# A weight-gradient matmul on one core: one load in four pieces, whole stores, a split last visit and a new hand-written order

## The chip, the cores and the metric

The kernel runs on one core of a Trainium2 chip. The core has five engines that run side by side, each through its own list of instructions: TensorE (PE in the profile; its weight loads are PEld) multiplies matrices into PSUM, VectorE (DVE) and ScalarE (ACT) add, copy and round, GpSimd (POOL) here adds a little and issues loads that change the number format, and SyncE (SP) issues plain transfers. Sixteen DMA engines move data between the chip's large memory (HBM) and the core's SBUF. PSUM has eight banks, and a matmul of this kernel fills three quarters of one.

The metric is the device time of one execution in microseconds (us); lower is better. The runs before took 161.19, 161.51 and 161.19 us.

## The reference

```python
batch, m, k, n = 16, 512, 1024, 768
# input [batch, m, k] and grad_output [batch, m, n], float32
grad_weight = np.einsum('bmk,bmn->kn', input, grad_output)   # [k, n] = [1024, 768]
```

With X the input as an 8192 x 1024 matrix and G the gradient as 8192 x 768, the result is X-transposed times G: a sum over 8192 rows. 58.7 MB are read and 3.1 MB are written.

## The kernel before

**Tiles.** The rows are cut into 64 slices of 128. X's columns are two halves of 512, each four quarters of 128 (q = 0 to 3); G's are two halves of 384 (LEFT, RIGHT). A product of one quarter (128 x 128, the weights) and one half of G (128 x 384) is one matmul of 384 columns, the only shape of line L331. The result's four blocks are A (first half of X, LEFT), B (first, RIGHT), C (second, LEFT) and D (second, RIGHT), each in four quarters.

**Two kinds of load.** The first eight slices (kind "s") are multiplied plainly, 16 matmuls a slice. The other 56 go in 28 pairs of slices (kind "P"), where VectorE makes sums and differences of the half tiles (`sum_x`, `sum_g`, lines L184 to L198), so that seven products (A, B, C, 1, 5, 6, 7) replace eight: 28 matmuls a pair. In all 8 x 16 + 28 x 28 = 912 matmuls. Products 1, 5, 6 and 7 are collected in their own sums (`macc`) and added to the blocks at the end.

**Loads.** Nearly all loads are issued by POOL (L153, L154, L158, L160) and rounded to bfloat16 on the way. Slice 0 and the X part of slice 1 come as float32 over the hardware queues: G's halves (`gf`) from SP (L128, L130), X of slice 0 (`xf[0]`) and of slice 1 (`xf[1]`) from ScalarE's queue (L129, L131). `round_by` (L202) then rounds them, partly on VectorE, partly on ScalarE; the tokens `r0` to `r4` place five of these: r0 is the right half of G of slice 0 (VectorE), r1 and r2 are quarters of X of slice 1 (VectorE), r3 and r4 the others (ScalarE). Meanwhile TensorE runs 17 warm-up matmuls on constants (L136).

**The order by hand.** The scheduler is off for TensorE, VectorE, ScalarE and POOL. `PLAN`, a list of some 1200 tokens, gives the order, and each engine runs its own tokens in that order:

- `C0@2.1`: begin block C, quarter 0, in bank 2 and run one matmul; `C0.1` runs one more there. `@R` means the block's own resident bank (5, 6, 7 for A0, A1, A2). Such a stretch in one bank is called a visit.
- `fB1@1`: fill bank 1 with what B1 has so far (ScalarE copy, L309), so that the next visit adds to it.
- `vB1`, `cB1`, `kC1`: close the visit. `v` is VectorE (a copy L376, an add L378, a last add L371 or L364 and L366), `c` a ScalarE copy to SBUF (L356), `k` an add by VectorE that folds D in (L360).
- `g0.4`, `x0.4`: stages of the sums of pair 4.
- `pA3`, `qA0`: POOL adds the shared sum (L388); `q` stores the block after it.

A bank can be begun or filled again only when the engine that closes it has read it. A closing with a last add stores its block: `store` (L285 to L291) issues one transfer of 128 x 384 (192 KB) on SP's queue, or, for the first four stores (`HALVED`), two of 96 KB. There are 16 such blocks, so 20 transfers.

Of the kernel before, what the change touches and what calls it, by code (L numbers as in the profile page):

```python
# [9 lines left out]
P = 128  # L10
# [4 lines left out]
    "C0@2.1 A0@R.1 r0 r1 r3 B1@1.1 r2 A2@R.1 r4 A1@R.1 vB1 A1.1 D3@4.2 A0.1 C0.1 D0@3.1 B2@0.1 cC0 B2.1 D0.1 "  # L15
    "fB1@1 A2.1 B3@2.2 cD3 B1.2 B3.1 D2@4.1 cB1 D2.1 vB3 D2.1 D0.1 A0.1 C1@2.3 C2@1.4 A1.2 cC2 B2.1 C1.1 B2.1 "
    "D2.1 cC1 D1@1.2 vD2 D1.1 fD3@2 D1.1 A2.2 cD0 vD1 B0@4.1 D3.2 A3@3.2 cD3 A3.2 B0.2 vA3 B0.1 C3@1.4 B2.2 "
    "B1@3.1 B0.1 cB2 B0.1 A1.2 cB0 D2@0.2 A0.3 D0@2.3 C3.2 A2.1 C0@4.1 vC3 C0.3 B1.2 B3@1.5 B1.1 D0.1 C0.1 vB1 "
    "C0.1 A0.2 vB3 D0.1 fD3@3 D2.2 vC0 fC3@1 A2.3 vD0 fD1@4 D3.3 vD2 D3.1 D1.1 g0.4 D1.1 fC1@0 D1.2 C3.1 fA3@2 "
    "g1.4 C3.1 C1.1 vD1 cD3 C1.3 kC3 fC2@3 A3.2 g2.4 A3.1 fB2@1 A3.1 x0.4 A3.1 C2.2 cA3 C2.1 x1.4 C2.2 A2.1 "  # L20
    "x2.4 10@2.1 cC2 A0.1 C1.1 v10 12@4.1 60@3.1 cC1 B2.1 g0.5 B2.1 c12 B2.1 61@0.1 g1.5 c60 62@2.1 B0@4.1 vB2 "
    "B0.1 c61 B0.1 11@3.1 c62 A1.1 vB0 A1.1 f12@1 A1.1 13@0.1 x0.5 13.1 12.1 11.1 c13 73@4.1 x1.5 73.1 c11 "
    "50@2.2 c12 k73 51@0.1 53@3.1 c50 53.1 x2.5 A1.1 52@4.1 g0.6 c53 52.1 51.1 fB1@2 A0.1 v52 63@1.2 c51 "
    "71@3.1 g1.6 71.1 fC0@4 g2.5 B1.2 g2.6 B1.1 c63 70@0.1 k71 70.1 C0.1 f10@1 C0.1 x0.6 C0.1 c70 B3@3.2 A1.1 "
    "cC0 10.1 x1.6 10.1 cB1 72@0.1 vB3 72.1 c10 72.1 C1@4.1 x2.6 f62@3 C1.1 60@2.1 k72 60.1 cC1 61@1.2 g0.7 "
    "A0.1 fB2@4 62.1 v61 62.1 B0@0.2 c62 g1.7 B2.2 vB0 c60 C3@1.2 cB2 C3.1 g2.7 C2@3.2 x0.7 fA3@2 C2.1 12@0.1 "
    "f51@4 12.1 vC3 A3.2 cC2 A3.1 v12 51.2 cA3 70@1.1 x1.7 70.1 c51 53@0.1 g0.8 53.1 A2.1 c70 A2.1 x2.7 A2.1 "
    "fB3@2 A1.1 v53 63@4.1 fB1@1 63.1 B3.1 g1.8 B3.1 f11@3 13@0.1 v63 13.1 cB3 B1.2 g2.8 11.1 v13 C3@4.1 cB1 "
    "C3.1 A2.1 x0.8 fC1@2s 11.2 C0@1.1 f71@0 C0.1 vC3 C1.2 cC0 71.1 x1.8 71.1 c11 71.1 vC1 52@1.2 c71 52.1 "
    "g0.9 A1.1 f73@3 60@4.2 v52 50@2.1 f62@0 50.1 g1.9 50.1 f13@1 73.1 v60 73.2 c50 62.1 x2.8 62.1 72@4.1 g2.9 "  # L30
    "72.1 c62 10@2.1 x0.9 10.1 c73 10.1 13.2 f70@0s v10 A0.2 f51@3 A0.1 v72 70.2 c13 51.1 x1.9 51.1 fC2@4s "
    "61@2.1 v70 61.1 fB2@1 61.1 C2.1 x2.9 C2.1 c51 B0@0.1 g0.10 B0.1 c61 B0.1 B2.1 vC2 B2.1 f11@3 B2.1 A2.1 "
    "vB0 f71@4 A3@2.2 x0.10 A3.1 cB2 11.1 A0.1 f12@0 11.1 g1.10 A2.1 71.1 f63@1 vA3 71.1 12.1 c11 12.1 g2.10 "
    "12.1 x1.10 c71 A1.2 g0.11 63.1 c12 63.2 fB1@4 x2.10 C1@3.2 g1.11 c63 62@2.2 vC1 B1.2 fB3@1 B1.1 v62 "
    "C0@0.1 fC3@3 C0.1 B3.1 g2.11 B3.1 cB1 B3.1 x0.11 C3.2 f72@4 C3.1 vC0 13@2.2 cC3 A2.1 x1.11 72.1 cB3 72.1 "
    "v13 72.1 f50@3s 73@0.2 g0.12 73.1 f53@1 52@2.2 v73 52.1 c72 50.2 g1.12 50.1 f60@0s 53.1 v52 53.1 fC0@4s "
    "53.2 g2.12 60.1 f51@2 v50 60.2 c53 A1.1 x0.12 A0.2 fB2@3 A1.1 C0.1 v60 f10@1 51.3 x1.12 C0.1 f70@0 10.2 "
    "vC0 c51 10.1 70.2 g0.13 70.1 f61@4s C2@2.2 x2.12 c70 C2.1 61.1 x2.11 c10 61.2 vC2 B2.2 f11@1 B2.1 g1.13 "
    "B0@0.1 f12@2 v61 B0.2 11.2 vB0 f62@4 11.1 12.2 cB2 x0.13 12.1 A3@0.1 c11 A3.2 g2.13 C1@3.1 f71@1 x1.13 "
    "C1.2 vA3 62.1 c12 62.2 g0.14 71.1 f63@0 71.2 x2.13 fC3@2 A2.1 63.1 vC1 63.1 c71 63.1 C3.1 g1.14 C3.1 c63 "  # L40
    "A2.1 g2.14 B3@1.1 c62 B3.2 x0.14 C3.1 A0.2 cC3 vB3 53@4.3 fB1@2 x1.14 73@0.2 v53 73.1 f72@1 50@3.2 x2.14 "
    "50.1 B1.1 v73 72.3 v50 60@4.2 c72 60.1 g0.15 B1.1 f52@0 B1.2 v60 13@3.3 A1.1 f70@4 x0.15 A1.2 cB1 52.2 "
    "v13 52.2 70.1 g1.15 70.1 c52 x1.15 70.1 A2.1 fC2@3 A2.1 g2.15 C0@0.1 g0.16 C0.1 c70 C0.1 C2.1 fB2@2 x2.15 "
    "C2.2 vC0 B0@4.2 cC2 B2.1 g1.16 B2.2 fC1@3 g2.16 51@1.2 vB0 51.1 cB2 12@0.2 x0.16 12.1 f10@4 C1.3 v51 10.2 "
    "cC1 10.1 x1.16 10.1 61@2.1 v12 61.1 c10 61.2 x2.16 f11@1 A1.1 71@0.1 g0.17 71.1 fB3@4 71.1 v61 62@3.3 v71 "
    "B3.3 v62 53@2.2 cB3 B1@0.1 g1.17 B1.1 11.1 v53 11.3 vB1 f60@2 A3@4.3 x0.17 c11 A3.1 A2.1 f72@3 A2.1 vA3 "
    "50@0.1 70@1.2 g0.18 72.1 f13@4 72.1 50.1 x1.17 50.1 72.1 v70 13.2 c72 13.1 g1.18 60.2 g2.17 c13 60.1 v50 "
    "63@1.1 fB2@3 63.2 g2.18 63.1 f73@0 A0.1 x0.18 A0.1 f52@4 A0.2 73.1 c60 x1.18 73.2 x2.17 73.1 52.1 x2.18 "
    "63.1 c73 C0@2.2 v63 C0.1 B0@0.2 vC0 B0.2 52.1 g0.19 52.1 fA3@2 A1.2 vB0 c52 B2.3 g1.19 f61@4 10@1.1 x0.19 "
    "10.2 A3.2 g2.19 51@0.2 x1.19 cA3 51.2 v10 cB2 A2.1 61.2 f62@2 v51 61.1 C1@3.2 x2.19 fC2@0 C1.1 62.1 g0.20 "  # L50
# [12 lines left out]
    "C2.2 vB0 C3@2.1 B2.1 A1.1 g1.27 fC0@4 A1.1 kC2 C3.3 g2.27 C3.1 f72@0 C0.2 x0.27 C0.3 vC3 71.3 kC0 72.1 "
    "fC1@2 72.2 vB2 72.1 fA3@4 72.2 x1.27 C1.2 c72 v71 C1.3 g0.28 f73@0 62@1.3 fB3@3 kC1 62.1 A0.1 73.1 g1.28 "
    "73.1 f51@2 v62 73.2 A3.1 g2.28 A3.2 x0.28 A3.1 52@1.2 cA3 51.1 x2.27 51.1 c73 51.1 x1.28 51.2 52.1 A1.1 "
    "50@0.1 v52 50.3 v51 61@4.1 f70@1 61.2 g0.29 61.2 70.1 g1.29 70.2 v61 70.1 A2.1 A1.1 v50 B3.1 f63@4 12@2.2 "
    "x0.29 12.1 63.3 x1.29 A2.2 g2.29 A2.1 70.1 x2.28 63.1 A0.1 v12 A0.2 B3.1 k70 B3.2 B1@0.1 x2.29 B1.1 cB3 "
    "B1.1 g0.30 B1.1 c63 B1.1 10@2.2 x0.30 f60@4 10.4 vB1 60.2 53@3.1 g1.30 53.2 x1.30 53.2 g2.30 13@0.2 v53 "
    "13.2 60.2 g0.31 f72@3 A1.2 f11@1 v10 A0.1 A2.1 72.1 g1.31 72.1 f12@2 72.1 11.1 g2.31 11.1 x2.30 11.2 "
    "x0.31 11.2 A1.1 13.1 c11 13.1 x1.31 12.1 cA1 12.1 v13 12.1 A0.1 f62@1 A2.1 x2.31 10@6.1 p63 c12 72.1 60.1 "  # L70
    "v10 cA2 62.3 cA0 62.1 v60 63@7.1 f73@6 63.1 qA0 v62 A3@0.1 f70@4 A3.1 73.1 v63 73.1 f50@5 73.2 qA2 v72 "
    "70.1 f53@2 A3.1 50.1 v73 70.1 fC3@3 53.1 50.1 v70 f61@1 qA1 50.1 C3.2 v53 fC2@7 C3.2 fB3@6 C3.1 pA3 61.2 "
    "cC3 61.1 v50 C2.1 f71@4 C2.3 qC3 f51@3 C2.1 v61 71.2 cC2 71.1 vA3 71.1 fC0@1 B3.1 qC2 B3.1 v71 B3.1 fB1@7 "
    "51.2 vB3 f52@0 51.1 C0.1 pC1 C0.1 fB0@4 v51 C0.2 fB2@5 C1@2.4 vC0 B1.2 52.1 vC1 52.2 vB1 B2.3 v52 B2.2 "
    "B0.4 vB2 B0.2 vB0 "
).split()

WARMUP = [("b", 512), ("f", 512), ("f", 512)] + 14 * [("b", 128)]
PAIRS_HELD = 11
SUMS_HELD = 8  # L80
MERGED = 2
HALVED = 4
ASIDES = 7
# [5 lines left out]
def kernel(  # L89
# [6 lines left out]
    nc = tc.nc  # L96
    bf16 = mybir.dt.bfloat16
    f32 = mybir.dt.float32
# [242 lines left out]
    def close(engine, p, q, queue):  # L341
# [39 lines left out]
        if last(p, q) and not opened[p, q] and not (engine == "c" and p in "ABC"):  # L381
            closed.add((p, q))
# [66 lines left out]
```

## Time and profile before

| what | value |
|---|---|
| runs, us | 161.19, 161.51, 161.19 (median 161.19) |
| profiled execution, us | 161.48 |
| its span (first to last instruction), us | 159.70 |
| granted TensorE clock | 0.999 |
| HBM read, over the span | 58.72 MB |
| TensorE: matmuls of L331, first and last start, us | 912; 5.91 and 155.75 |
| one whole VectorE closing (128x384), mean | 0.55 us |
| one ScalarE fill or closing, mean | 0.48 to 0.49 us |
| one POOL add (L388), mean | 1.0 us |
| SP's store issues, first to last end, us | 147.16 to 157.03 |
| issue to landing of a store, median, us | 2.1 (192 KB), 1.7 (96 KB) |

A row of the timeline or of the groups is one kind of instruction at one line: start, busy time, engine, line, operation, what it writes and reads, how many, and in brackets the idle time before it with what ended it. Matmuls overlap, so their busy time is longer than the step from one to the next. The row of a window gives, for each engine, the busy time and the number of instructions in that stretch, then the clock, the busy share of the DMA engines and what they moved. A cast load counts there with the bytes that it writes, which are half of those read.

### The profile page before, as it was taken

The page shows a single profiled execution, that of the slowest core. Times are in us where ns is not written, and L with a number is a line of the kernel's source. Part 1 is how long each engine was busy: PE and PEld are TensorE (multiplying, and loading weights), DVE is VectorE, ACT ScalarE, POOL GpSimd, SP SyncE. Part 2 cuts the span into 40 slices and gives each one's busy share as a digit, 9 for nine tenths or more (in the row PEclk, how much of TensorE's full clock was granted, in tenths as well). Part 3 has the DMA queues.
Part 4 walks back from the last instruction along what each step waited for, and adds up shares of the span by engine and source line. Part 5 has one row for each costly group of instructions (what it writes and reads, how often), then busy time and mean ns, then how long its engine had stood idle before and what let it go on. Part 6 is the DMA issues. An engine that isn't in the chain of part 4 may idle for free.

```text
span 159.7 us, 2734 instructions
## 1 busy us (share of the span) xinstructions
PE 154.6 (97%) x931; PEld 91.2 (57%) x931; DVE 136.1 (85%) x316; ACT 104.4 (65%) x243; POOL 42.6 (27%) x77
## 2 busy tenths in 40 slices
PE   8899999999999999999999999999999999999990
PEld 3456656556555565665656565656566565656560
DVE  0514169999999999999999999989999899999992
ACT  3445238999999999967867585563465472339930
POOL 7442222222212222221222221222222100006930
PEclk9999999999999999999999999999999999999999
DMA  5999999999999999999999999999999999940696
GB/s 171 297 212 211 214 216 212 213 213 212 213 213 211 214 212 213 214 211 214 213 214 212 214 213 214 212 211 213 213 211 219 208 214 213 213 81 0 196 353 239
DMA packets 12829, 33.40 MB, mean 209 GB/s; under 512 B 1424, under 2 KB 4624, under 8 KB 12816
## 3 DMA queue, kind: packets, MB, share of 16 engines
q0 software_dynamic: 9360, 28.64, 90.7%
q1 hardware_dynamic: 3168, 3.54, 6.6%
q10 hardware_dynamic: 288, 1.05, 1.7%
q8 instruction: 7, 0.11, 0.3%
q14 instruction: 6, 0.05, 0.1%
HBM read 58.72 MB, written 3.15 MB: 387 GB/s over the span
## 4 chain that ended last, share of the span: by engine, by line
PE 91%; DMA 4%; DVE 2%; issue 1%; ACT 0%; ACTq 0%; DVEq 0%
PE bank L331 91%; DMA xf<-in_input_dram 4%; DVE acc L371 1%; DVE macc L364 0%; DVE xp L202 0%; ACT macc L356 0%; ACTq L129 0%; DVE acc L378 0%; DVE acc L366 0%; DVEq L371 0%
## 5 line engine op out<-in xcount | busy, mean ns | idle before, releaser
L331 PE MATMUL bank<-gp,xp 128*128 128x384 bf16 x576 | 105.4, 326 | 0.7 <-DVE xp L202 0.6
L331 PEld LDWEIGHTS <-xp 128*128 128x128 bf16 x576 | 55.8, 98 | 39.1 <-DVE xp L202 1.0
L331 PE MATMUL bank<-ge,xe 128*128 128x384 bf16 x336 | 65.9, 326 | 0.0
L331 PEld LDWEIGHTS <-xe 128*128 128x128 bf16 x336 | 32.7, 98 | 22.3 <-DVE xe L184 0.6
L309 ACT COPY bank<-macc 128x384 f32<-128x384 f32 x69 | 32.6, 489 | 10.4 <-DVE macc L378 6.2
L356 ACT COPY macc<-bank 128x384 f32<-128x384 f32 x64 | 29.4, 484 | 10.4 <-PE bank L331 10.1
L378 DVE TENSOR_TENSOR macc<-bank,macc 128x384 f32<-128x384 f32 x56 | 30.5, 554 | 1.2 <-PE bank L331 0.9
L154 POOL DMA_DIRECT2D xp<-in_input_dram x30 | 15.9, 529 | 52.6 <-DMA xp<-in_input_dram 21.9
L309 ACT COPY bank<-acc 128x384 f32<-128x384 f32 x46 | 21.8, 485 | 11.5 <-DVE acc L378 8.9
L356 ACT COPY acc<-bank 128x384 f32<-128x384 f32 x44 | 20.7, 480 | 11.4 <-PE bank L331 11.1
L153 POOL DMA_DIRECT2D gp<-in_grad_output_dram x30 | 15.9, 531 | 38.4 <-PE bank L331 17.2
L378 DVE TENSOR_TENSOR acc<-bank,acc 128x384 f32<-128x384 f32 x42 | 22.8, 553 | 1.9 <-PE bank L331 1.9
L184 DVE TENSOR_TENSOR xe<-xp 128x1024 bf16<-128x1024 bf16 x28 | 19.3, 689 | 1.0 <-DMA xp<-in_input_dram 0.9
L194 DVE TENSOR_TENSOR ge<-gp 128x768 bf16<-128x768 bf16 x28 | 15.5, 552 | 0.2 <-DMA gp<-in_grad_output_dram 0.2
L376 DVE COPY acc<-bank 128x384 f32<-128x384 f32 x9 | 5.0, 555 | 8.9 <-PE bank L331 8.9
L186 DVE TENSOR_TENSOR xe<-xe,xp 128x512 bf16<-128x512 bf16 x28 | 11.8, 421 | 0.3
L188 DVE TENSOR_TENSOR xp<-xp,xe 128x512 bf16<-128x512 bf16 x28 | 11.5, 419 | 0.0
L196 DVE TENSOR_TENSOR ge<-gp,ge 128x384 bf16<-128x384 bf16 x28 | 9.9, 353 | 0.2
L198 DVE TENSOR_TENSOR gp<-ge,gp 128x384 bf16<-128x384 bf16 x28 | 9.8, 354 | 0.2
L388 POOL TENSOR_TENSOR acc<-acc,macc 128x384 f32<-128x384 f32 x7 | 6.8, 1003 | 0.5 <-ACT acc L356 0.5
L388 POOL TENSOR_TENSOR macc<-macc 128x384 f32<-128x384 f32 x1 | 1.0, 1042 | 18.0 <-DVE macc L378 18.0
L202 DVE CAST gp<-gf 128x192 bf16<-128x192 f32 (+1 forms) x2 | 0.6, 310 | 4.9 <-DMA gf<-in_grad_output_dram 4.9
(23 smaller groups left out, 41.2 us busy)
## 6 DMA issues: line engine op xcount, KB each, us to landing
xp<-in_input_dram POOLq DMA_DIRECT2D x30, 512.0 KB, 16.7
gp<-in_grad_output_dram POOLq DMA_DIRECT2D x30, 384.0 KB, 16.7
out_dram<-acc SPq DMA_DIRECT2D x12, 192.0 KB, 2.1
xf<-in_input_dram ACTq DMA_DIRECT2D x2, 512.0 KB, 4.9
out_dram<-acc SPq DMA_DIRECT2D x8, 96.0 KB, 1.7
gp<-in_grad_output_dram POOLq DMA_DIRECT2D x3, 192.0 KB, 6.4
xp<-in_input_dram POOLq DMA_DIRECT2D x2, 256.0 KB, 7.8
gf<-in_grad_output_dram SPq DMA_DIRECT2D x2, 192.0 KB, 4.1
```

The costliest lines, as they stand in the source:

```text
L153: nc.gpsimd.dma_start(out=gp, in_=G[rows, :].rearrange("(p m) n -> p m n", m=2))
L154: nc.gpsimd.dma_start(out=xp, in_=X[rows, :].rearrange("(p m) k -> p m k", m=2))
L184: nc.vector.tensor_sub(out=xe[:, 0:2, :], in0=x[:, 1::-1, :], in1=x[:, 3::-2, :])
L186: nc.vector.tensor_sub(out=xe[:, 2, :], in0=xe[:, 0, :], in1=x[:, 0, :])
L188: nc.vector.tensor_add(out=x[:, 1, :], in0=x[:, 2, :], in1=xe[:, 2, :])
L194: nc.vector.tensor_add(out=ge[:, 0:2, :], in0=g[:, 0:2, :], in1=g[:, 1::2, :])
L196: nc.vector.tensor_add(out=ge[:, 2, :], in0=g[:, 3, :], in1=ge[:, 0, :])
L198: nc.vector.tensor_add(out=g[:, 1, :], in0=ge[:, 2, :], in1=g[:, 2, :])
L309: nc.scalar.copy(out=tile_[:, at : at + c1 - c0], in_=src[:, c0:c1])
L331: nc.tensor.matmul(tile_[:, at : at + c1 - c0], stat, mov[:, c0:c1], start=fresh, stop=True, skip_group_check=True,)
L356: nc.scalar.copy(out=to, in_=b)
L378: nc.vector.tensor_add(out=to, in0=b, in1=to)
```

## The change

Five things are changed together.

1. X of slice 1 (`xf[1]`) is loaded in four transfers of 32 rows each, alternately on ScalarE's and SP's queue, instead of one of 128 rows on ScalarE's.
2. The first of the warm-up matmuls writes bank 4, the others bank 7; before, all wrote bank 7.
3. No store is halved (`HALVED = 0`).
4. The last visit, of B2, is split over two banks, 256 columns in bank 7 and 128 in bank 1 (`fB2@7+1`). Each part is closed and stored by itself, the first on SP's queue, the second on ScalarE's. The kernel before already had the code for such a visit, and did not use it at the end.
5. `PLAN` is another order of the same 912 matmuls. It has 128 instead of 129 VectorE closings by `v`, 119 instead of 115 ScalarE closings, 124 instead of 122 fills, six `q` and two `p` instead of five and three. Three lines of `close` allow a ScalarE closing of a block that POOL has prepared; no token of the new order needs them.

```diff
 PLAN = (
-    "C0@2.1 A0@R.1 r0 r1 r3 B1@1.1 r2 A2@R.1 r4 A1@R.1 vB1 A1.1 D3@4.2 A0.1 C0.1 D0@3.1 B2@0.1 cC0 B2.1 D0.1 "
...
-    "70.1 f53@2 A3.1 50.1 v73 70.1 fC3@3 53.1 50.1 v70 f61@1 qA1 50.1 C3.2 v53 fC2@7 C3.2 fB3@6 C3.1 pA3 61.2 "
-    "cC3 61.1 v50 C2.1 f71@4 C2.3 qC3 f51@3 C2.1 v61 71.2 cC2 71.1 vA3 71.1 fC0@1 B3.1 qC2 B3.1 v71 B3.1 fB1@7 "
-    "51.2 vB3 f52@0 51.1 C0.1 pC1 C0.1 fB0@4 v51 C0.2 fB2@5 C1@2.4 vC0 B1.2 52.1 vC1 52.2 vB1 B2.3 v52 B2.2 "
-    "B0.4 vB2 B0.2 vB0 "
+    "A0@R.1 C2@2.1 A3@3.1 A2@R.1 cC2 A1@R.1 vA3 C0@1.1 C1@0.1 vC1 r3 r0 r2 D2@4.1 r1 D2.1 vC0 B0@2.2 B1@0.2 "
+    "cB0 D1@1.2 r4 C3@3.3 D2.1 A1.1 cC3 A1.1 vD2 A2.1 cB1 A2.1 B3@2.2 fC1@0 B3.1 C0@3.2 fA3@4 C1.2 vC0 C1.1 "
...
+    "f72@6 61.1 qA2 61.1 v70 50.1 cA0 50.2 f52@0 v61 53.1 72.1 fB3@7 72.1 qC0 v50 72.2 fC3@3 52.2 B3.1 f71@5 "
+    "B3.1 v72 qA0 C3.1 fC2@2 C3.2 v53 C3.1 cB3 C3.1 71.1 f51@4 71.1 qB3 71.1 v52 cC3 71.2 C2.1 fB2@7+1 C2.2 "
+    "qC3 C2.1 v71 C2.1 fC1@0 51.2 vC2 fB1@3 51.1 C1.2 v51 fB0@6 C1.2 B1.2 B0.2 vB1 B0.3 vC1 B0.1 B2.2 vB0 B2.5 "
+    "vB2 "
 ).split()
...
-HALVED = 4
+X1_PARTS = 4
+HALVED = 0
...
-    nc.scalar.dma_start(out=xf[1], in_=X[P : 2 * P, :])
-
-    wps = psum.tile([P, 512], f32, name="bank7")
-    for dt, cols in WARMUP:
+    if X1_PARTS == 1:
+        nc.scalar.dma_start(out=xf[1], in_=X[P : 2 * P, :])
+    else:
+        n = P // X1_PARTS
+        for b in range(X1_PARTS):
+            engine = nc.scalar if b % 2 == 0 else nc.sync
+            engine.dma_start(out=xf[1][b * n : (b + 1) * n, :], in_=X[P + b * n : P + (b + 1) * n, :])
+
+    warm = [psum.tile([P, 512], f32, name=f"bank{b}") for b in (4, 7)]
+    for n, (dt, cols) in enumerate(WARMUP):
         dtype = f32 if dt == "f" else bf16
         nc.tensor.matmul(
-            wps[:, 0:cols],
+            warm[min(n, 1)][:, 0:cols],
...
+                assert (p, q) not in prepared or (final and carried and len(parts) == 1)
...
-        if last(p, q) and not opened[p, q] and not (engine == "c" and p in "ABC"):
+        if final and engine == "c" and (p, q) in prepared:
+            store(p, q, 0, NH, queue)
+        if last(p, q) and not opened[p, q] and (engine != "c" or p not in "ABC" or (p, q) in prepared):
             closed.add((p, q))
```

Between the removed and the added lines that end the list, the last visit before is B0's with two matmuls and one closing; after, it is B2's with five matmuls in each of two banks.

## The prediction

> **What bounds the kernel now.** I read the page's busy shares first, then windows of the span, then single waits on the timeline, then the stores.
>
> ```profile
> PE 154.6 (97%) x931; PEld 91.2 (57%) x931; DVE 136.1 (85%) x316; ACT 104.4 (65%) x243; POOL 42.6 (27%) x77
> ```
>
> TensorE has 97%. The 912 matmuls of L331 start between 5.91 and 155.75 us, and nearly all steps from one to the next in the trace are 162 or 163 ns: 911 steps of 0.1626 are 148.13 of 149.84 us. So 1.71 us is idle, and a new order can only win there and at the two ends. The windows (busy us and count of PE, PEld, DVE, ACT, POOL; clock, DMA share, GB/s) show a second bound:
>
> ```profile
> 2.00:3.00 1.00, 1.00 (x3) 0.46 (x2) 0.00 (x0) 0.95 (x1) 1.00 (x3) 1.00 0.87 254
> 3.00:4.00 1.00, 1.00 (x3) 0.35 (x2) 0.00 (x0) 0.00 (x0) 1.00 (x2) 1.00 1.01 407
> 6.00:7.00 1.00, 0.96 (x7) 0.30 (x4) 0.36 (x1) 0.00 (x0) 0.00 (x0) 1.00 1.13 241
> 12.00:40.00 28.00, 28.00 (x174) 16.52 (x174) 20.33 (x45) 19.67 (x47) 6.86 (x13) 1.00 1.07 213
> 120.00:140.00 20.00, 20.00 (x124) 11.85 (x123) 18.75 (x46) 9.05 (x21) 1.58 (x3) 1.00 1.07 213
> ```
>
> From 3 us until the last load lands (142.53 by the landing record of that load) the 16 DMA engines are never free. TensorE runs just behind them, and the idle spots show it:
>
> ```profile
> 7.70 20.16 PE L331 MATMUL bank<-gp,xp 128*128 128x384 bf16 x123 [0.62 <-DVE xp L202]
> ...
> 11.92 15.55 PEld L331 LDWEIGHTS <-xp 128*128 128x128 bf16 x97 [0.21 <-DMA xp<-in_input_dram]
> ...
> 51.79 0.60 PEld L331 LDWEIGHTS <-xp 128*128 128x128 bf16 x5 [0.34 <-DMA xp<-in_input_dram]
> ...
> 88.41 0.48 ACT L356 COPY macc<-bank 128x384 f32<-128x384 f32 x1 [0.62 <-PE bank L331]
> ...
> 125.73 0.69 DVE L184 TENSOR_TENSOR xe<-xp 128x1024 bf16<-128x1024 bf16 x1 [0.70 <-DMA xp<-in_input_dram]
> ```
>
> In steps over 0.1626, the idle 1.71 us is: 0.78 before the sixth matmul (slice 1) and 0.20 before the third (right half of G of slice 0); 0.12 at 51.5 and 0.16 at 126.2 behind loads; the remaining 0.45 where a bank or a sum came late (0.15 at 40.1, 0.25 at 88.5, small ones).
>
> Then the end, where nothing but stores is left:
>
> ```profile
> 149.00:150.00 1.00, 1.00 (x8) 0.61 (x7) 1.00 (x4) 1.00 (x4) 1.00 (x3) 1.00 0.65 206
> 150.00:151.00 1.00, 1.00 (x8) 0.59 (x7) 1.00 (x4) 1.00 (x4) 0.98 (x2) 1.00 0.65 207
> 152.00:153.00 1.00, 1.00 (x9) 0.59 (x7) 1.00 (x3) 1.00 (x3) 1.00 (x2) 1.00 1.02 364
> 156.00:157.00 1.00, 0.08 (x1) 0.00 (x0) 0.65 (x2) 0.00 (x0) 0.00 (x0) 1.00 1.02 363
> 157.00:158.00 1.00, 0.00 (x0) 0.00 (x0) 0.00 (x0) 0.00 (x0) 0.00 (x0) 1.00 1.03 369
> ```
>
> The halved stores move 206 GB/s; the whole ones fill the DMA engines from 152 to 158.3. The eight halves leave SP at 147.16 to 150.43, about 0.48 apart; whole ones at 151.00 to 154.90, about 0.49 apart. 192 KB at 366 GB/s is 0.54 us, so whole stores land 0.54 apart, and the last at 158.80: 151.00 + 1.35 until data flow + 12 x 0.54 = 158.8. So the last 7 us hang on the store stream from 151.0 on, and the last adds of VectorE only have to keep up with it.
>
> **The change, part by part.** Sum against the profiled execution's 161.48 us (span 159.70, 1.78 around it). The runs shown have a median of 161.19, so this execution lies 0.29 above it.
>
> *Opening.* The built order on TensorE is seven matmuls of slice 0 with the left half of G, then D2, which needs the right half. VectorE rounds that half (r0) only behind two copies of banks, of A3 (third matmul) and C1 (seventh). First matmul at 5.91 (it follows the warm-up, whose 17 matmuls are unchanged; one of them writes another bank and no later instruction comes sooner by that: 0). C1 starts 6 x 0.1626 later, at 6.89; a VectorE reader of a bank starts 0.36 after the matmul's start (last one: 155.75 to 156.12): 7.25; r0 follows at the pitch of 0.465 of such copies: 7.72, ends 0.36 later (row of the 128x384 rounding): 8.08; D2 8.10. Behind r0 wait r2, r1 and the copy of C0; TensorE needs them at 8.4, 9.1 and 9.1 and has them at 8.3, 8.5 and 9.0. In the kernel before the eighth matmul starts at 8.03: +0.07. Then the 31st matmul, at 8.10 + 23 x 0.1626 = 11.84, needs slice 3, which landed at 11.88: +0.06. Opening: +0.13, in place of the waits of 0.78 and 0.20.
>
> *X of slice 1 in four.* It landed at 7.12. Now r2 is at its turn at 7.99 and ScalarE's r3 is needed by 7.8, so an earlier landing wins nothing and up to 0.6 later costs nothing itself. The bytes, and the 16 engines, are the same, with a share of 1.01 to 1.16 already in 3 to 8 us; two more issues of 0.43 each lie on SP (empty until 147) and on ScalarE, whose table load then ends at 3.4, before its first rounding at 4.22. I take 0 for the loads behind it. Below: 0 too, since the free share of 2 to 3 us lies before any piece could start. Above: 512 KB at 400 GB/s are 1.3 us; at half that rate, 1.3 us more.
>
> *New order.* It has the same 912 matmuls, one VectorE closing less, two ScalarE fills and four ScalarE closings more. I counted where each load is first needed, at 0.1626 a matmul. The load of 51.75 is first used by the 276th matmul instead of the 275th, that of 125.70 by a VectorE sum nine matmuls later (736th against 727th): -0.28. Tightest now is the load of 47.44, due 47.42 with the opening's shift: +0.05. Late banks and sums: 0.45 before, not countable by slack; bounds 0 and 0.9, I take 0.45, since closings and fills number nearly the same and ScalarE (65% busy) has room for six copies of 0.48. Middle: -0.23.
>
> *Last visit split.* B2's last seven matmuls become seven of 256 and seven of 128 columns. The last 128-column matmuls of the warm-up start 57 ns apart, its 14 cost 96 ns on average; 256 columns lie between 57 and 163 (110 taken). The last start moves from 6 x 0.163 to 7 x 0.110 + 6 x 0.058 behind the visit's first: +0.14 (up to +0.4 at 96). What it shortens, the last add and store, is hidden by the store stream: without that cover the add of 0.55 would fall to some 0.25.
>
> *No store halved, new end.* Behind B3's last matmul come 30 whole matmuls and B2's 14 parts, so it starts 31 x 0.1626 + 1.12 = 6.16 before the last start, T. ScalarE copies B3 after 0.36 + 0.38 (behind a fill) in 0.48, POOL adds in 1.0 (its rows: 1003 ns), SP stores 0.03 later: T - 3.91. Ten stores' worth (nine whole, one in 128 + 64 KB) follow, all ready when SP gets to them at 0.49 apart: T - 3.91 + 1.35 + 10 x 0.54 = T + 2.84. Before, the last landing was 158.80 - 155.75 = 3.05 behind the last start: -0.21. The four stores made whole save 4 x 0.47 us of SP, but POOL's adds, 1 us apart, hide most of that.
>
> Sum: +0.13 - 0.23 + 0.14 - 0.21 = -0.17, so 161.31 against the profiled execution; from the median, without the late load that other executions need not have (-0.16), it is 161.19 + 0.16 - 0.17 = 161.18. I take **161.2 us**: no change. One measurement can tell about 0.2% (0.32 us) from none, so this means 160.87 to 161.51.
>
> **Rivals.** *Pieces of 32 rows load slowly (slower).* Each piece writes a quarter of the partitions. If that goes at half rate, and two of the four pieces find no other transfer to run beside, 0.65 us of the load stream is lost. For: the share above 1 leaves nothing to make it up, and loads are used as they land: slice 2 (9.63) is due 9.72, slice 3 has no slack. Against: every transfer of the trace has 128 rows, so no row shows it. It decides from 0.1 us on: 161.2 + 0.65 - 0.1 = 161.75, up to 162.4.
>
> [...]
>
> *The new order hands banks over later (slower).* VectorE is busy 85% and stays so; twice the 0.45: 161.65. Against: as many closings.
>
> *The new order has no late banks (faster).* TensorE then follows the loads: the last, at 142.53, is first used by the 834th matmul, 78 steps and the split before T: 142.55 + 12.68 + 0.14 = 155.37, last landing 158.21, 0.59 less than 158.80; 160.6 to 160.9 after the two reference times: 160.75. For: the order is set by load times everywhere else. Against: the wait at 88.4 came with a copy whose matmul was long done, which no order excludes.
>
> **How the numbers follow.** Forecast 0.40, slow pieces 0.26, late banks 0.10, no late banks 0.24. So faster 0.24, the same 0.40, slower 0.36. The range takes the fast case and most of the slow pieces: 160.7 to 161.9; the forecast's own is 160.87 to 161.51.
>
> **What would show it.** Right: the eighth matmul at 8.1 behind r0; X of slice 1 landed before 7.8 and that wait gone from the chain; loads of slices 2 and 3 at 9.6 and 11.9; no wait at 126; DMA share 1.0 from about 152 to 158, last landing 2.8 to 2.9 behind the last matmul's start. Wrong: slices 2 and 3 later by 0.2 or more (slow pieces), an eighth matmul before 7.8, idle TensorE over 0.9 us in the middle, or a share under 0.9 in the last 5 us, which would put the end back on the last add.

## The result, and the profile after

The changed kernel took 162.37 us (median of 12 executions, beside 161.38 for the kernel before): 1.0069 times as long, interval 1.0055 to 1.0083. A second series gave 162.30 against 161.38, 1.0060 (1.0046 to 1.0074). It is slower by 0.6 to 0.7%, above the forecast of 161.2 and outside its range.

The first profiled execution, of 164.81 us, has a disturbance of its own: TensorE's clock fell to 0.50 for 3.4 us. Two of the first twelve executions (163.92 and 164.81) show a lower mean clock (0.985 and 0.99), the other ten (0.995 to 1.00) take 162.07 to 162.41. TensorE's rows on its timeline, and its windows (columns as in the prediction):

```profile
5.75 1.60 PE L338 MATMUL bank<-gp,xp 128*128 128x384 bf16 x7 [0.50 <-DVE xp L209]
8.27 0.32 PE L338 MATMUL bank<-gp,xp 128*128 128x384 bf16 x1 [0.91 <-DVE gp L209]
10.13 4.62 PE L338 MATMUL bank<-gp,xp 128*128 128x384 bf16 x17 [1.54 <-ACT xp L209]
```

```profile
9.00:10.00 1.00, 0.00 (x0) 0.00 (x0) 0.29 (x1) 0.33 (x1) 0.53 (x1) 1.00 1.14 209
...
11.00:12.00 1.00, 1.00 (x4) 0.45 (x3) 0.00 (x0) 0.61 (x2) 0.53 (x1) 0.50 1.14 213
12.00:13.00 1.00, 1.00 (x4) 0.45 (x3) 0.00 (x0) 0.04 (x1) 0.53 (x1) 0.50 1.12 217
13.00:14.00 1.00, 1.00 (x5) 0.46 (x4) 0.56 (x1) 0.97 (x3) 0.53 (x1) 0.50 1.10 217
```

Seven matmuls, a wait, one matmul, a longer wait, and then four matmuls per us instead of eight at a clock of 0.50. The fall costs 1.7 us (eleven steps of 0.32 instead of 0.163). Whatever is said of the change from here on is read from an execution of the second series, 162.26 us at a clock of 0.995. Its page and its timeline:

```profile
span 160.4 us, 2757 instructions
...
PE 153.9 (96%) x938; PEld 92.0 (57%) x938; DVE 136.4 (85%) x316; ACT 107.5 (67%) x250; POOL 42.5 (26%) x77
...
PE bank L338 92%; DMA xf<-in_input_dram 4%; DVE acc L379 0%; SPq L138 0%; SPq L131 0%; ACT xp L209 0%; SPq L129 0%; DVEq L454 0%; ACTq L209 0%
```

```profile
5.68 1.30 PE L338 MATMUL bank<-gp,xp 128*128 128x384 bf16 x7
...
7.89 0.32 PE L338 MATMUL bank<-gp,xp 128*128 128x384 bf16 x1 [0.91 <-DVE gp L209]
8.80 0.41 ACT L209 CAST xp<-xf 128x256 bf16<-128x256 f32 x1 [2.12 <-DMA xf<-in_input_dram]
8.84 0.50 DVE L209 CAST xp<-xf 128x256 bf16<-128x256 f32 x2 [1.00 <-DMA xf<-in_input_dram]
...
9.26 0.66 PE L338 MATMUL bank<-gp,xp 128*128 128x384 bf16 x3 [1.04 <-ACT xp L209]
```

The chain of waits, in order of time, shows the same from the other side, first in the kernel before, then in the changed one:

```profile
1.18 5.94 DMA xf<-in_input_dram
7.12 0.02 issue
7.14 0.51 DVE xp L202 x2
```

```profile
1.65 0.42 SPq L138
2.07 0.04 issue
2.11 6.53 DMA xf<-in_input_dram
...
8.80 0.41 ACT xp L209
9.22 0.05 issue
9.26 34.55 PE bank L338 x211
43.81 0.03 issue
43.83 112.53 PE bank L338 x695
```

In the kernel before, the whole tile lands at 7.12. In the changed one SP issues its first piece at 1.65 to 2.07 (the first row) and its second, the last of the four, from 2.11 on; that one lands at 8.64. VectorE and ScalarE stand idle until then (the 1.00 and 2.12 in brackets) and round it, and the ninth matmul starts at 9.26. From there TensorE runs almost without a stop to the end: the time is lost once, in the first 10 us. The ninth matmul starts 1.06 us later than in the kernel before (8.20) and the last one 0.65 later; the difference is later waits that the new order does not have.

| landings and starts, us | before | changed | changed, first profile |
|---|---|---|---|
| right half of G of slice 0 | 6.00 | 6.42 | 7.06 |
| X of slice 1 whole | 7.12 | 8.64 | 9.51 |
| X of slice 2, of slice 3 | 9.63, 11.88 | 10.28, 12.48 | 10.94, 13.14 |
| last matmul starts | 155.75 | 156.41 | 158.96 |
| last store lands | 158.80 | 159.42 | 161.98 |
| end of the span | 159.71 | 160.39 | 162.95 |

### The profile page after: what moved, and what is told of

The parts are those of the page before. It is cut to its first block, busy times and chain, and to the rows that moved or that the text cites. A ratio compares the mean times of both kernels' runs of the same rounds, so it can differ in the third digit from the quotient of the medians.

```text
span 162.9 us, 2757 instructions
## 1 busy us (share of the span) xinstructions
PE 155.3 (95%) x938; PEld 92.4 (57%) x938; DVE 136.3 (84%) x316; ACT 107.6 (66%) x250; POOL 42.6 (26%) x77
## 4 chain that ended last, share of the span: by engine, by line
PE 91%; DMA 5%; SPq 1%; DVE 0%; issue 0%; ACT 0%; DVEq 0%; ACTq 0%
PE bank L338 91%; DMA xf<-in_input_dram 5%; DVE acc L379 0%; SPq L138 0%; SPq L131 0%; ACT xp L209 0%; SPq L129 0%; DVEq L454 0%; ACTq L209 0%
## 5 line engine op out<-in xcount | busy, mean ns | idle before, releaser
L338 PE MATMUL bank<-gp,xp 128*128 128x384 bf16 (+2 forms) x583 | 106.5, 328 | 3.1 <-ACT xp L209 1.5
L338 PEld LDWEIGHTS <-xp 128*128 128x128 bf16 x583 | 57.2, 99 | 41.9 <-ACT xp L209 3.4
L338 PE MATMUL bank<-ge,xe 128*128 128x384 bf16 x336 | 64.9, 326 | 0.0
L316 ACT COPY bank<-macc 128x384 f32<-128x384 f32 x66 | 31.3, 487 | 11.2 <-DVE macc L386 6.8
L386 DVE TENSOR_TENSOR macc<-bank,macc 128x384 f32<-128x384 f32 x59 | 32.1, 552 | 2.4 <-PE bank L338 1.8
L364 ACT COPY macc<-bank 128x384 f32<-128x384 f32 x62 | 28.8, 483 | 7.9 <-PE bank L338 7.3
L316 ACT COPY bank<-acc 128x384 f32<-128x384 f32 (+2 forms) x52 | 24.6, 482 | 12.4 <-DVE macc L386 7.1
L364 ACT COPY acc<-bank 128x384 f32<-128x384 f32 x50 | 23.3, 481 | 11.1 <-PE bank L338 10.8
L386 DVE TENSOR_TENSOR acc<-bank,acc 128x384 f32<-128x384 f32 x40 | 21.9, 553 | 8.6 <-PE bank L338 8.5
L384 DVE COPY acc<-bank 128x384 f32<-128x384 f32 x8 | 4.4, 553 | 4.2 <-PE bank L338 4.1
L379 DVE TENSOR_TENSOR macc<-bank,macc 128x384 f32<-128x384 f32 x7 | 3.7, 551 | 0.0
```

The lines of the kernel that those rows point to most:

```text
L316: nc.scalar.copy(out=tile_[:, at : at + c1 - c0], in_=src[:, c0:c1])
L338: nc.tensor.matmul(tile_[:, at : at + c1 - c0], stat, mov[:, c0:c1], start=fresh, stop=True, skip_group_check=True,)
L364: nc.scalar.copy(out=to, in_=b)
L386: nc.vector.tensor_add(out=to, in0=b, in1=to)
```

## The experiments

Times are medians with the ratio to the kernel before and its 95% interval. "End" is the time from the last landing to the end of the span in the run's profile; what sets it is told with the last group.

| kernel | us | ratio (interval) | end |
|---|---|---|---|
| before | 161.35 to 161.40 | | 0.91 |
| changed | 162.37, 162.30 | 1.0069 (1.0055 to 1.0083), 1.0060 (1.0046 to 1.0074) | 0.97 |
| e1: changed, X in one piece | 161.51 | 1.0009 (1.0001 to 1.0018) | 1.15 |
| e2: before, X in four pieces | 164.56 | 1.0180 (1.0148 to 1.0212) | 1.21 |
| e3: changed, every fourth row in a piece | 162.09 | 1.0041 (1.0028 to 1.0054) | 0.98 |
| e4: changed, pieces of 256 columns | 164.68 | 1.0178 (1.0150 to 1.0206) | 0.97 |
| e5: changed, all pieces on ScalarE's queue | 162.66 | 1.0080 (1.0067 to 1.0093) | 1.08 |
| e6: one piece, on SP's queue | 162.19 | 1.0048 (1.0035 to 1.0061) | 1.15 |
| e8: one piece, r0 earlier | 161.57 | 1.0010 (1.0002 to 1.0019) | 1.15 |
| e9: one piece, four stores halved | 162.42 | 1.0064 (1.0051 to 1.0077) | 1.35 |
| e10: one piece, last visit whole; again: e19 | 161.23; 161.44 | 0.9988 (0.9979 to 0.9996); 1.0002 (0.9993 to 1.0010) | 1.15 |
| e12: before, whole stores | 161.80 | 1.0025 (1.0016 to 1.0034) | 1.15 |
| e13: e12 and the last visit split | 161.94 | 1.0033 (1.0020 to 1.0046) | 1.15 |
| e14: changed, two pieces of 64 rows | 162.50 | 1.0068 (1.0054 to 1.0082) | 1.10 |
| e15: e10 with four tiny loads; again: e20 | 161.13; 161.00 | 0.9986 (0.9978 to 0.9995); 0.9983 (0.9974 to 0.9992) | 0.91 |
| e16: before with one tiny load | 161.83 | 1.0030 (1.0019 to 1.0041) | 1.35 |
| e17: changed, two pieces of every second row | 161.89 | 1.0032 (1.0020 to 1.0044) | 1.03 |

### The four pieces alone

The pieces taken out of the changed kernel, and put alone into the kernel before.

```diff
 # e1, from the changed kernel
-X1_PARTS = 4
+X1_PARTS = 1
 # e2, from the kernel before
-    nc.scalar.dma_start(out=xf[1], in_=X[P : 2 * P, :])
+    n = P // 4
+    for b in range(4):
+        engine = nc.scalar if b % 2 == 0 else nc.sync
+        engine.dma_start(out=xf[1][b * n : (b + 1) * n, :], in_=X[P + b * n : P + (b + 1) * n, :])
```

> The changed kernel with X of slice 1 in one transfer of 128 rows again; order, stores, split visit and warm-up stay changed. Theory (pieces of 32 neighbouring rows load at half rate and make every load behind them late): X of slice 1 lands at about 7.1 us, slice 3 at about 11.9, and the time is 161.2 us (160.9 to 161.5), the sum of the prediction. Rival (the new order costs the time, the pieces nothing): 162.2 to 162.5.

> The kernel before with nothing changed but X of slice 1 in four pieces of 32 neighbouring rows over both queues. Theory (the late landing of X of slice 1 stops TensorE): its order needs that tile at the sixth matmul, three matmuls sooner than the changed kernel (ninth), so it loses more: 162.6 to 163.4 (before 161.35), sixth matmul at about 10. Rival (the pieces cost the same everywhere, by the load stream): plus 0.9, 162.2 to 162.4. Rival (the new order makes the pieces dear): 161.4 to 161.7.

In one piece the new order takes 161.51, 0.86 below the changed kernel; the tile lands at 7.09 and the ninth matmul has no wait:

```profile
4.79 1.08 PE L143 MATMUL bank<-const-bfloat16-1.0 128*128 128x128 bf16 x12
5.71 1.30 PE L338 MATMUL bank<-gp,xp 128*128 128x384 bf16 x7
7.92 2.79 PE L338 MATMUL bank<-gp,xp 128*128 128x384 bf16 x15 [0.91 <-DVE gp L209]
```

In the kernel before, the pieces cost 3.2 us in the median. One of its six executions took 162.84 at a clock of 1.00, as expected (its profile: tile whole at 8.73 for 7.12, last landing 1.05 later); the other five took 164.2 to 164.9 at a clock of 0.99, above the 162.6 to 163.4 expected. So the pieces delay the last landing by 1.05 us in the old order and by 0.95 in the new one (159.42 for 158.47), and cost 1.7 more in executions at the lower clock. Whether TensorE's longer stops (1.07 and 1.93 us here) are what lowers it was not shown: no run changes the stops alone. Nearly the whole result is this one edit.

### Why the pieces are slow: rows, columns, queues

```diff
 # e3 (with 4 written for X1_PARTS) and e17 (X1_PARTS = 2), from the changed kernel
-            engine.dma_start(out=xf[1][b * n : (b + 1) * n, :], in_=X[P + b * n : P + (b + 1) * n, :])
+            engine.dma_start(out=xf[1][b::X1_PARTS, :], in_=X[P + b : 2 * P : X1_PARTS, :])
 # e4
+            w = K // X1_PARTS
+            engine.dma_start(out=xf[1][:, b * w : (b + 1) * w], in_=X[P : 2 * P, b * w : (b + 1) * w])
 # e5
-            engine = nc.scalar if b % 2 == 0 else nc.sync
+            engine = nc.scalar
 # e6, with X1_PARTS = 1
-        nc.scalar.dma_start(out=xf[1], in_=X[P : 2 * P, :])
+        nc.sync.dma_start(out=xf[1], in_=X[P : 2 * P, :])
 # e14
-X1_PARTS = 4
+X1_PARTS = 2
```

> The changed kernel, its four pieces still of 32 whole rows and on the same two queues, but each takes every fourth row, so that it writes partitions from the whole range. [...] Rival 1 (four small transfers cost by their number): as the changed kernel, 162.2 to 162.5. Rival 2 (two hardware queues take the share of GpSimd's loads): 162.2 to 162.5.

> The changed kernel with four pieces of all 128 rows and 256 columns each, on the same two queues. Theory (neighbouring partitions): X of slice 1 lands by 7.6, time 161.2 to 161.6 (packets of 1 KB may be less efficient). Rivals (number of transfers, two queues): 162.2 to 162.5.

> The changed kernel with its four pieces of 32 neighbouring rows all on ScalarE's queue. [...] Rival (two queues): 161.2 to 161.5.

> The changed kernel with X of slice 1 in one transfer of 128 rows, but on SP's queue behind both halves of G. Theory (the third transfer of a queue starts late and then shares the engines with GpSimd's loads): packets of 4 KB at 160 to 180 ns, but a landing of 7.6 to 8.6 instead of 7.1, 161.5 to 162.1. Rival (only the neighbouring partitions make a piece late): a landing of 7.1 and 161.5, as with one piece on ScalarE's queue.

> The changed kernel with X of slice 1 in two pieces of 64 neighbouring rows, one on each hardware queue: one transfer more than in one piece, and only SyncE's queue has a third. If neighbouring rows are the trouble and 64 are no better than 32, packets of 4 KB take 200 us/1000 or more each (0.20 to 0.35 us, against 0.16 to 0.17 for 128 rows and for strided rows) and the tile is whole at 8.3 or later: 162.0 to 162.6. If only the number of transfers in a queue counts, packets stay at 0.16 to 0.18 us, the half on SyncE lands near 8.0 as the single piece did there, and the time is at most 162.2.

> The changed kernel with X of slice 1 in two pieces as in the two halves of 64 neighbouring rows, but each piece takes every second row, so that each spreads over all 128 partitions' range. Same number of transfers and bytes in each queue as the two halves (162.50; SyncE's packets 265 ns, tile whole at 8.55, 1.18 us of wait before the ninth matmul). If neighbouring rows cost the time, packets are back at 160 to 175 ns, the tile is whole 0.3 to 0.8 earlier and the time is 161.9 to 162.2. If the third transfer of a queue costs it whatever its rows are, it stays at 162.4 to 162.6.

From the DMA records of each trace (median time of a packet in each piece of X of slice 1 and its landing, pieces in the order of the program; packets of 4 KB but for e4; "changed" is the second series):

| kernel | packet, ns | pieces land, us | ninth matmul waits, us |
|---|---|---|---|
| before; e1: one piece of 128 rows, ScalarE's queue | 159; 159 | 7.12; 7.09 | none (e1) |
| e6: one piece, SP's queue | 172 | 8.01 | 0.61 |
| e17: two pieces of every second row | 159, 172 | 6.42, 8.11 | 0.11 |
| e3: four pieces of every fourth row | 159, 172, 159, 172 | 5.53, 7.42, 8.41, 8.48 | 1.02 |
| e14: two pieces of 64 neighbouring rows | 175, 265 | 7.19, 8.55 | 1.18 |
| changed: four pieces of 32 neighbouring rows | 159, 182, 233, 212 | 6.08, 7.79, 8.35, 8.64 | 1.21 |
| e5: the same on one queue | 159, 204, 203, 244 | 6.29, 7.32, 8.40, 9.03 | 1.64 |
| e4: four pieces of 256 columns | 46, 59, 46, 59 (1 KB) | 6.21, 8.72, 8.87, 10.37 | 2.62 |

Two things are told apart. First the rows: e14 and e17 have the same transfers, bytes and queues, and differ only in which rows a piece takes. With neighbouring rows a packet of SP's piece takes 265 ns, with every second row 172, and the time is 162.50 against 161.89. ScalarE's piece shows when: of its 64 packets in e14 the 32 that end before GpSimd's loads begin (5.21) take 159 ns, the other 32 take 327. In e17 the later ones take 231, and in e1, in one piece, 159 throughout. So in e14 the neighbouring rows were slow beside other transfers (327 ns) and not before them (159). TensorE's rows of the two, e14 first:

```profile
7.68 0.32 PE L338 MATMUL bank<-gp,xp 128*128 128x384 bf16 x1 [0.92 <-DVE gp L209]
9.03 1.64 PE L338 MATMUL bank<-gp,xp 128*128 128x384 bf16 x9 [1.02 <-ACT xp L209]
```

```profile
6.07 1.33 PE L338 MATMUL bank<-gp,xp 128*128 128x384 bf16 x7
8.31 2.47 PE L338 MATMUL bank<-gp,xp 128*128 128x384 bf16 x13 [0.92 <-DVE gp L209]
```

The wait for ScalarE's rounding, 1.02 in e14, is gone from e17's rows: its matmuls go on from 8.31 with a gap of only 0.11, too small to end the row. Part of that is e17's later eighth matmul; the ninth starts at 8.59 in e17 and at 9.03 in e14.

Beside other transfers the later pieces take 182 to 244 ns a packet with 32 neighbouring rows and 265 with 64, against 159 to 172 for a tile of 128; with every fourth row they are back at 159 to 172. Why neighbouring rows are slower there was not shown.

Second, cutting and queuing cost something of their own: e4, from which 161.2 to 161.6 was expected, took 164.68, and e3 162.09, where one piece (e1) takes 161.51. Pieces with packets as short as before still make the tile late (8.11 in e17, 8.48 in e3), and so does the whole tile when it is SP's third transfer (8.01 in e6). In the traces of e3, e14 and e17 the first packet of SP's third transfer starts 0.56 to 0.78 us after the last data packet of the second has ended, in e4 0.38 after; in e2, e6 and the changed kernel it starts before that end. In e6 GpSimd's loads begin at 4.44 instead of 5.19 (e1) and share the engines with it. e4 spreads over all 128 rows and is the latest of all: 1 KB in 46 to 59 ns is 4 KB in 184 to 236. Each piece in e5 takes 0.6 to 1.1 us behind the one before. What delays a third transfer in some kernels was not settled.

Apart from the "end" the pieces cost 162.37 - 161.51 + (1.15 - 0.97) = 1.04 us in the changed kernel, and strided pieces 162.09 - 161.51 + 0.17 = 0.75 (four) or 161.89 - 161.51 + 0.12 = 0.50 (two; 0.68 by the mean spans, which come up under "Stores and the end"). So half a microsecond or more is cutting and queuing, and 0.2 to 0.3 (four pieces: 162.30 or 162.37 less 162.09) to 0.5 (two: 162.50 - 161.89, less 0.07 of end) is neighbouring rows. The median of e4 holds the fall of the clock: its profile, at a clock of 1.00, is of 163.62 us, and four of six executions, at 0.99 or less, took 164.6 and more.

### The wait for r0 in the opening

```diff
 # e8, from e1
-    "A0@R.1 C2@2.1 A3@3.1 A2@R.1 cC2 A1@R.1 vA3 C0@1.1 C1@0.1 vC1 r3 r0 r2 D2@4.1 r1 D2.1 vC0 B0@2.2 B1@0.2 "
+    "A0@R.1 C2@2.1 A3@3.1 A2@R.1 cC2 A1@R.1 r0 vA3 C0@1.1 C1@0.1 vC1 r3 r2 D2@4.1 r1 D2.1 vC0 B0@2.2 B1@0.2 "
```

> One piece of 128 rows on ScalarE's queue as in e1_one_piece (161.51), and the rounding r0 ahead of VectorE's copies of A3 and C1, so that the eighth matmul no longer waits 1.08 us. Theory (TensorE follows the loads of slices 2 and 3 anyway): the wait moves to those loads, 161.3 to 161.6. Rival (the wait is on the path to the end): 160.5 to 160.9.

161.57, the same as e1. The wait before the eighth matmul falls from 1.08 to 0.30, but 0.53 appears before the ninth and 0.11, 0.17 and 0.43 before the 11th, 14th and 18th; the 31st, which needs slice 3 (landed at 12.03, in e1 at 11.90), starts at 12.07 for 11.95 in e1. In this opening TensorE follows the loads, and the 0.78 us taken away before the eighth matmul only moved.

### Stores and the end

```diff
 # e9, from e1
-HALVED = 0
+HALVED = 4
 # e10 (and e19), from e1
-    "B3.1 v72 qA0 C3.1 fC2@2 C3.2 v53 C3.1 cB3 C3.1 71.1 f51@4 71.1 qB3 71.1 v52 cC3 71.2 C2.1 fB2@7+1 C2.2 "
+    "B3.1 v72 qA0 C3.1 fC2@2 C3.2 v53 C3.1 cB3 C3.1 71.1 f51@4 71.1 qB3 71.1 v52 cC3 71.2 C2.1 fB2@7 C2.2 "
 # e12, from the kernel before; e13 has the second edit too
-HALVED = 4
+HALVED = 0
-    "51.2 vB3 f52@0 51.1 C0.1 pC1 C0.1 fB0@4 v51 C0.2 fB2@5 C1@2.4 vC0 B1.2 52.1 vC1 52.2 vB1 B2.3 v52 B2.2 "
+    "51.2 vB3 f52@0 51.1 C0.1 pC1 C0.1 v51 fB0@4+3 C0.2 fB2@5 C1@2.4 vC0 B1.2 52.1 vC1 52.2 vB1 B2.3 v52 B2.2 "
```

> As e1_one_piece, but the first four stores halved again. Theory (the store stream sets the end, and SP issues halves at 0.48 us each): the ten last stores start 0.4 later, 161.9 (161.7 to 162.1). Rival (the end is set by the last matmul and add): 161.5, no change.

> X of slice 1 in one piece again, and the last visit (B2 of step 31) not split: seven matmuls of 384 columns at the end, one add and one store of 192 KB. If the split's extra matmuls set the end (my term of +0.14 on the last start), the time falls by about 0.1 below that of the one-piece kernel, 161.4. If the store stream from the store of B3 on sets the end, the earlier last start wins nothing, and one whole store behind one whole add of 0.55 ends 0 to 0.3 us later: 161.5 to 161.8.

> The kernel before with no store halved and nothing else changed. If halved stores cost the end something in that order too (eight halves at 206 GB/s ahead of twelve whole stores at 366), the last landing comes some 0.3 us closer to the last matmul's start (before: 3.05) and the time is 161.0 to 161.2 where the kernel before has 161.4. If POOL's adds, 1 us apart, set the end of these stores, it stays at 161.4 within 0.1.

> The kernel before with no store halved and its last visit, B0, split into 256 and 128 columns in two banks. If the store stream still binds, the split adds its 0.14 us to the last start and wins nothing: within 0.1 of the same kernel unsplit. If the last add and its store bind once the stores are whole, the shorter last add (0.25 for 0.55) and the smaller last store win 0.1 to 0.3: 160.8 to 161.1.

In the new order halving costs 0.91 us (162.42 against 161.51), of which 0.20 is "end". Windows from e1, then from e9:

```profile
149.00:150.00 1.00, 1.00 (x8) 0.61 (x7) 1.00 (x3) 1.00 (x3) 1.00 (x2) 1.00 0.83 297
150.00:151.00 1.00, 1.00 (x8) 0.61 (x7) 1.00 (x3) 1.00 (x4) 0.61 (x2) 1.00 0.81 294
151.00:152.00 1.00, 1.00 (x8) 0.60 (x7) 1.00 (x3) 1.00 (x4) 1.00 (x2) 1.00 0.91 330
...
158.00:159.00 1.00, 0.00 (x0) 0.00 (x0) 0.00 (x0) 0.00 (x0) 0.00 (x0) 0.93 0.01 1
```

```profile
149.00:150.00 1.00, 1.00 (x8) 0.61 (x7) 1.00 (x4) 1.00 (x3) 1.00 (x2) 1.00 0.64 206
150.00:151.00 1.00, 1.00 (x8) 0.61 (x7) 1.00 (x3) 1.00 (x4) 0.60 (x2) 1.00 0.64 204
151.00:152.00 1.00, 1.00 (x8) 0.61 (x7) 1.00 (x3) 1.00 (x4) 1.00 (x2) 1.00 0.62 199
...
158.00:159.00 1.00, 0.00 (x0) 0.00 (x0) 0.00 (x0) 0.00 (x0) 0.00 (x0) 1.00 0.64 226
```

In both kernels SP issues a store every 0.4 to 0.6 us, half or whole. In e9 it has 20 issues from 147.40 on and no pause, and the last leaves 1.18 behind the last matmul's start, later than any add is due. In e1 SP has 16 issues, pauses for POOL three times and the last leaves 0.58 behind (0.63 for the part on ScalarE's queue).

In the old order whole stores go the other way, against what was expected: 161.80 for 161.40. 0.24 of the 0.40 is "end", and 0.10 is a later last landing. There the last store leaves 0.95 behind the last matmul's start with halves and without, because the last add sets it; whole, the stream loses its steady pace (pauses of SP at 149.6 to 151.1 and at 151.5 to 152.2) and the last landing comes 3.14 instead of 3.05 behind. So halved stores paid in the order that they were chosen for, by little without the "end"; the remaining 0.06 is not told apart from noise. The split (e13, which also closes product 51 ahead of the fill) did not help there either: the last landing is 3.07 behind the start, the median 161.94, and e12's interval overlaps e13's.

Without the split (e10) the new order takes 161.23 and, on another chip, 161.44 (e19), for 161.51 with it. The last landing lies 3.03 us behind the last matmul's start in both, for 3.05 with it; that start is 0.22 earlier in e10's profile, and 0.09 later in e19's, where X of slice 1 lands at 7.40 and slice 3 at 12.27 (11.90 in e1). Split, the last two stores land 0.48 and 0.65 behind the one before them; whole, the last lands 0.50 behind. That is 0.14, and the medians say 0.07 to 0.28.

The time outside the span takes part in this. The record has each execution's span too, to 0.1 us. Time less span is 1.75 to 1.80 us in the mean of most kernels, the one before among them, but 1.94 in e1, 1.92 to 1.99 in e6, e8 and e9, 1.86 to 1.89 in the changed kernel and e3. By mean spans e10 is 0.11 below e1 and e19 0.03 above it. So the split costs some 0.1 us inside the span at most, and why e1 and its kin have 0.16 more outside it stays open: e13, e14 and e17 are split too and have 1.75 to 1.79.

### The end: SyncE's waits

e1 has its last landing 0.33 us before that of the kernel before, but its span ends only 0.09 earlier. After the last landing the trace has these instructions of SyncE (start from the last landing, semaphores waited for; left the kernel before, right e12):

```
-0.494  117 112            -0.511  110 102
+0.017  118 113            +0.016  111 101
+0.082  114                +0.076  115 100
                           +0.137  116 99
                           +0.196  117 112
                           +0.258  118 113
                           +0.323  114
```

At the end of these two programs SyncE waits for the DMA semaphores one after another, in the same order in both, 0.06 us a wait. The DMAs of the two hardware queues take eight of them in turn. With 24 such DMAs (before) the last store has the eighth, 118, and one short wait follows. With 20 (e10, e12) it has the fourth, 111, and four more waits come ahead of that one. That is the "end" of the table: 0.91 for the eighth, 0.97 for the seventh, 1.15 for the fourth, 1.35 for the first. Only e5 does not fit: its last landing has the seventh, with the same waits behind it, and its end is 1.08, by a longer last step.

```diff
 # e15 (and e20) from e10, four of them; e16 from the kernel before, one of them
+    tiny = accp.tile([1, 4, 16], f32, name="tiny")
+    for b in range(4):
+        nc.sync.dma_start(out=tiny[:, b, :], in_=X[b : b + 1, 0:16])
```

> The one-piece, unsplit kernel (161.23 measured) with four added loads of 64 bytes on SyncE's queue behind the right half of G; nobody reads them. At the program's end SyncE waits for the DMA semaphores in pairs, always in the same order, 0.06 us a wait; the hardware queues' DMAs take eight of these semaphores in turn, so the number of DMAs says at which wait of the list the last store comes. With 20 DMAs it is the fourth of eight and four waits follow; with 24, as in the kernel before, it is the last. If these waits cost what they seem to, the span ends 0.91 behind the last landing instead of 1.15 and the time is 0.24 lower: 161.0, faster than the kernel before (161.4) by 0.4. If the waits are not on the path, or the tiny loads cost the opening something, the time stays at 161.2 or rises to 161.4.

> The kernel before with one added load of 64 bytes on SyncE's queue behind the right half of G; nobody reads it. 25 DMAs instead of 24: the last store then takes the first of the eight semaphores, and seven waits of 0.06 us follow its landing. If the order of the waits counts: 0.43 slower, 161.8, with 1.34 us between the last landing and the span's end instead of 0.91. If not: 161.4, same as the kernel before within 0.1.

> The changed kernel once more, for a profile in which TensorE's clock doesn't fall. If the fall of the clock to 0.5 between 11 and 14 us in its first profile was an addition of that execution, this one gives 162.1 to 162.4 and a span of about 160.4, with X of slice 1 whole at 8.5 or later, 4 KB packets of its pieces at 200 ns or more on SyncE's queue, and 0.97 us from the last landing to the span's end. If the clock belongs to the change, it gives 163 or more.

> The one-piece, unsplit kernel again, on the same chip as the next one: 161.1 to 161.4, 1.15 us from the last landing to the span's end.

> The same with the four tiny loads, on the same chip. 0.91 us from the last landing to the span's end. If the tiny loads cost the opening nothing, it is 0.24 below the one without them; it was 0.10 below on another chip, so if they cost 0.14 there, it is 0.05 to 0.15 below.

One unread load of 64 bytes makes the kernel before 0.47 us slower (161.83 for 161.36, 0.43 expected): its last landing is where it was (158.81 for 158.80), and the end is 1.35 for 0.91. Four of them make e10's end 0.91 for 1.15. The time showed 0.10 of that 0.24 across two chips and 0.44 on one chip (161.00 for 161.44); the mean is 0.27. The four tiny loads make up for the four DMAs that e10 has fewer than the kernel before. This kernel is the best of the study, and below the kernel before in both series: 0.9986 (0.9978 to 0.9995) and 0.9983 (0.9974 to 0.9992), a gain of about 0.3 us.

e18 is the second series of the changed kernel: 162.30, its profile at 162.26 with the clock at 0.995. The fall of the clock belongs to single executions, not to the usual cost of the change.

## Why the prediction was wrong

**X of slice 1 in four: this step failed.** It held that "an earlier landing wins nothing and up to 0.6 later costs nothing itself", and took 0. The landing was later by 1.5 us (8.64 for 7.12), beyond the 0.6 that was free, and the ninth matmul waited 1.21. The step counted bytes and the share of the DMA engines; it left open how long a packet takes when its rows lie side by side, and what stands ahead of a third transfer in a queue. Its range, 0 to 1.3, holds the measured 1.04; the value taken was the wrong end.

**The rival "pieces of 32 rows load slowly" was the case**, with a chance of 0.26. No run shows the half rate that it set for pieces of 32 rows: their later pieces took 182 to 244 ns a packet in the median for 159, 1.1 to 1.5 times as long. In e14, with 64 rows, the packets of the first piece beside other transfers took twice as long (327 for 159). The rival's 0.65 us on the load stream came out too, X of slice 2 landing 0.65 late and slice 3 0.60, but partly by luck: with every fourth row and short packets (e3) slice 2 is still 0.42 late. And it looked for the damage there. The damage came by the tile itself, whose lateness alone holds TensorE past the time when slices 2 and 3 have landed; and half or more of it is not the rows but the cutting. So 161.75 was too low, its upper end of 162.4 about right.

**Opening.** Right: the eighth matmul waits behind r0, 1.08 in e1 for 1.05 worked out (8.10 - 5.91 - 7 x 0.1626). The 31st starts at 11.95 in e1 for 11.84.

**New order.** Too cautious. The 0.45 of late banks and sums was kept; after the 31st matmul e1 has single waits of 0.14 in all and e10 of 0.07, where the kernel before has 0.73 (0.28 of it behind loads). The last matmul of e1 starts at 155.43; the sum put it 0.04 behind the 155.75 of the kernel before. The rival "no late banks" had this right, and its 155.37 for the last start is within 0.06.

**Last visit split.** Its parts run as worked out (109 to 110 ns for 256 columns, 55 to 56 for 128, 57 taken), so the last start moves by 0.13 for 0.14. The last add, of 128 columns, took 0.28 us in the first profile, for the 0.25 estimated.

**No store halved, new end.** Mis-sized: the last landing is 3.05 behind the last start, not 2.84. B3's store leaves 3.78 before it, not 3.91 (0.13); it lands 1.91 later for 1.89 (0.02), and the last landing lies 4.91 behind that for 9 x 0.54 = 4.86 (0.05). Together these undo the 0.21. The pitch of 0.49 and the share of 1.0 held, and POOL's adds hid nothing of what halves cost in this order (0.71 without the end).

**What was not in the sum at all** is the end behind the last landing: 0.24 us in e1, whose last landing has the fourth semaphore where that of the kernel before has the eighth, and 0.06 in the changed kernel, where the three more loads bring it to the seventh. The time outside the span was a constant in the sum, 1.78; in e1 it is 1.94.

So in e1's profile: -0.33 at the last matmul, 0 at the last landing behind it, +0.24 at the end, -0.09 in the span, where the sum said -0.17. That profile of the kernel before holds 0.16 of late load that, as the sum allowed, others need not have: in the mean e1's span is that of the kernel before (159.58 and 159.59), and the +0.16 of the medians (1.0009, interval 1.0001 to 1.0018) lies outside it. All but the pieces came out as next to no change, which was the forecast; the pieces are the result. The forecast's base of 161.19, from three executions, was also some 0.2 below the 161.35 to 161.40 of the later series; that is no part of the mechanism.

## What to carry to other kernels

Cutting a load that an engine waits for early into groups of neighbouring rows cost 1.04 us here: cost a piece by its own landing, from how its rows lie, what runs beside it and what stands ahead of it in its queue, not by its bytes alone. Before a store stream at the end is changed, ask which of three sets the end (the issuing queue's pitch, the data rate or the last add), since whole stores won 0.7 us in one order and lost 0.1 to 0.16 in the other (both without the stretch behind the last landing), and ask what follows the last landing. When profiles of two kernels are compared, subtract the stretch behind the last landing: here it moved by up to 0.44 us with the mere number of transfers; and compare the time outside the span, which differed by up to 0.2.

## What the runs showed of the hardware

- Packets of 4 KB to 32 or 64 neighbouring partitions took 182 to 270 ns in the median of a later piece beside other transfers (changed, e5, e14; 327 in e14's first piece, once GpSimd's loads had begun) and 159 before; to 128 partitions 159 to 172 (before, e1, e6).
- The last waits of the program went through the DMA semaphores one after another at 0.06 us each, and one unread load of 64 bytes cost 0.47 us (e16: 161.83 for 161.36, the end 1.35 for 0.91).
- TensorE's clock fell to 0.50 in one profile after a stretch (7.2 to 10.1 us) with a single matmul, stayed there from 10.8 to 14.2 and cost 1.7 us. What made it fall was not shown. The mean clock is lower (0.985 and 0.99) in 2 of 16 executions of the changed kernel, and in e2 five of six, with a clock of 0.99, lie 1.39 us or more above the sixth.
- SP's third transfer began 0.38 to 0.78 us after its second had moved its last data in four kernels (e3, e4, e14, e17), and before that in three (e2, e6, the changed one); why was not found.
